# A decoder layer on one core: copies moved between two queues, the attention stage reordered, one load and one split earlier, and four down-projection inputs split ahead of the last up tile

## The chip, the cores and the metric

The kernel runs on one core of a Trainium2 chip. The metric is the device time of one execution in microseconds (us); lower is better. The engines are named as the profile names them: PE is TensorE, DVE is VectorE, ACT is ScalarE, POOL is GpSimd, SP is SyncE, which only issues DMAs here. Each engine works through its own queue in order and meets the others by semaphores.

## The reference

One layer of a hybrid decoder, 256 tokens of width 2048, in float32. Cut to what matters:

```
ada = silu(c) @ w_ada + b_ada                 # 2048 -> 6 vectors of 2048
sh_m, sc_m, gt_m, sh_f, sc_f, gt_f = split(ada, 6)
h = rmsnorm(x, g_pre_mix) * (1 + sc_m) + sh_m
q, k, v, u = split(h @ w_in)                  # 1024, 128, 128, 1024 columns
attn = sliding_window_attention(q, k, v, sinks)   # 16 heads, window 128
y = s5_ssm(u, ...)                            # a complex diagonal recurrence over time
z = gelu(y);  ssm = z * sigmoid(z @ w_glu)
mix = concat(rmsnorm(attn), rmsnorm(ssm)) @ w_out
x = x + (1 + gt_m) * rmsnorm(mix, g_post_mix)
h = rmsnorm(x, g_pre_ffn) * (1 + sc_f) + sh_f
val, gate = split(causal_conv3(h @ w_up))     # 2 x 5632 columns
ff = (gelu(gate) * val) @ w_down
x = x + (1 + gt_f) * rmsnorm(ff, g_post_ffn)
```

## The kernel before

The kernel goes through five stages: the input projection (A), the attention and recurrence stage, the gate and output projection, the up projection, the down projection. All weights stream from HBM through six buffers of 128 x 2048 floats (`raw`); SP issues these loads in the order of the program, and each waits until a buffer is free.

**Precision.** Output, up and down projections are done as three products of a high and a low part: `split(hi, lo, src, e)` casts on ScalarE (`hi`) and subtracts on VectorE, or on POOL if the second letter of `e` is g (`lo`). `hl` does this for half a weight tile (128 x 1024). In the profile the parts are h_wout and l_wout, h_wup and l_wup, h_wdn and l_wdn; fh and fl are those of a down-projection input.

**Order.** In the attention stage and up to the first up tiles the program writes the order of VectorE, ScalarE, POOL and TensorE out by hand (class `in_order`, whose call stands at line 72, so most instructions there carry L72). After `s1m.close()` a planner orders these four engines; only SP keeps the program's order.

**The attention stage.** `B(k4, kk...)` does the second half of the query projection, 64 matmuls in all over four weight tiles (16 calls of 4 matmuls, each run in two passes); `q_tiles` copies the result out. For each of eight head pairs hp: `att_scores(hp)` (TensorE), `att_max(hp)` (VectorE finds the masked maximum, ScalarE does the exponentials), `att_norm(hp)` (a tiny reciprocal on VectorE, then four scalings on ScalarE), `pv(hp)` (TensorE transposes, ScalarE copies to pT), `att_out(hp)` (TensorE, then a ScalarE copy out of PSUM bank 7). Beside it runs the recurrence: `scan(n)` does the next n of ten steps on VectorE, `x2_half` copies the states, `y_mu(yb)` and `y_cx(yb)` are its two products into one PSUM bank, `y_out(yb)` copies that out, and `z_part(n)` transposes it and applies the Gelu on ScalarE.

Also beside it, the adaLN vectors are computed: `do()` is one sum of 128 x 2048 products on VectorE (line 142) and then a `pump()`; `pair()` does two tiles with TensorE into bank 7 and copies the partial sums out (`part`); `cols()` sums these with a few matmuls in the same bank and copies two columns to `ada`. `pump(n)` issues the next n loads of a fixed list (adaLN tiles, gate weights). Both copies are on ScalarE.

**Output projection.** The loop over k loads w_out tiles and adaLN tiles, splits, multiplies, and does one or two `do()`. At k = 9 it issues the load of x1's first half, at k = 13 that of the second half and of the first up tiles. The last three k are held back, so that the banks finish one after the other.

**Start of the up projection.** Residual and norm are done in quarters (`sq`, `gain`, `x_add`), the result is transposed (`x_turn`), scaled (`x_scale`) and split (`x_split`) into h2, four tiles h2A and h2B in the profile. In between stands the split of the last half of the second up tile, `ups[1].append(hl_half(wu1, 1))`.

**Up and down projection.** 44 pairs of up tiles (`up_tile`) give 44 inputs `ffa[:, f]`. The first eleven get their shift later, by `late_sum`, which uses a row broadcast in the buffer with the tag "cbc"; the last `late_sum` runs at f = 32. The down projection then takes each f: load, split of ffa into fh and fl (tags y0 and y1, three buffers each, shared with the up tiles), split of the two weight halves, 24 matmuls.

Of the kernel before, what the change touches and what calls it, by code (L numbers as in the profile page):

```python
# [59 lines left out]
def decoder_layer(ctx: ExitStack, tc: tile.TileContext, i, out):  # L60
# [524 lines left out]
    def pair():  # L585
        (vec, m, t0), (_, _, t1) = pair_in.pop(0), pair_in.pop(0)
        ps = bank(7, "ps_ada")
        ada_mm((t0, t1), ps)
        pump(2)
        part = parts[:, npair[0] % 3]  # L590
        npair[0] += 1
        A.copy(part, ps[:, :2 * P])
        pairs.append((ps[:, 2 * P:2 * P + 2], part, vec * KD + m))

    def cols():
        res, part, o = pairs.pop(0)
        ada_cols(part, 2, res)
        A.copy(ada[:, o:o + 2], res)


    accB = []
# [174 lines left out]
    def att_norm(hp):  # L776
        st, s_ = ast[:, hp], prob[hp]
        V.tensor_add(st[:, :, 2:4], st[:, :, 2:4], st[:, :, 4:6])
        V.reciprocal(st[:, :, 2:4], st[:, :, 2:4])
        for h2 in range(2):  # L780
            for b, bs in ((0, slice(0, P)), (1, slice(P, 3 * P))):
                act_scale(s_[:, h2, bs], s_[:, h2, bs], st[:, h2, 2 + b:3 + b])

    def pv(hp, heads=(0, 1)):
        s_ = prob[hp]
        pT = pts.setdefault(hp, [])
        for h2 in heads:
            psp = bank((4, 3 if hp < 4 else 4 if hp < 6 else 6)[h2], "ps_p")
            for b in range(3):
                PE.transpose(psp[:, b * P:(b + 1) * P], s_[:, h2, b * P:(b + 1) * P], ident)  # L790
            pT.append(p2.tile([P, 3 * P], F32, tag="pT", name="pT", bufs=2))
            A.copy(pT[h2], psp[:, :3 * P])
# [102 lines left out]
    def B(k4, *kks):  # L895
        for kk in kks:
            mm_winb(k4, kk)
# [23 lines left out]
    pv(1)  # L921
    att_scores(2)
    B(1, 1)
    scan(2)
    att_max(2)
    att_out(1)
    B(1, 2, 3)
    pump()
    scan(2)
    att_norm(2)  # L930
    B(2, 0)
    pv(2)
    att_scores(3)
    scan(2)
# [5 lines left out]
    x2_half(0)  # L940
    x2_half(1)
    att_max(3)
    B(3, 0)
    y_mu(0)
    B(3, 1)
    att_norm(3)
    B(3, 2)
    do()
    pv(3)
    B(3, 3)  # L950
    pump()
    pair()
    q_tiles(2, A.copy)
    q_tiles(3, V.tensor_copy)
    y_cx(0)
    y_out(0)
    cols()
# [19 lines left out]
    y_out(2)  # L977
    att_out(4)
    att_scores(7)
    pair()  # L980
    z_part(0)
    pv(5)
# [2 lines left out]
    y_block(3, (0, 1))  # L985
    att_norm(6)
    att_out(5)
    att_max(7)
    y_block(3, (2, 3))
    y_out(3)  # L990
    pair()
# [137 lines left out]
    for k in range(3, KD):  # L1129
        while len(outs_) < min(k + 3, KD):  # L1130
            ld_out()
            ld(2 if k in (4, 6, 8) else 1)
        while nw < min(2 * k + 6, 2 * KD):
            out_hl(nw)
            nw += 1
        out_proj(k, 0)
        out_proj(k, 1)
        if 3 < k < 8:
            ssm_half(2 * k - 8)
        for _ in range(2 if k in (5, 7, 9) else 1):  # L1140
            if ada_in:
                do()
        if k == 9:

            x1 = [ld_x("x1", 0)]
        elif k == 13:
            wu0, wu1 = (raw(i["w_up"][0, vg], 2048, "wup") for vg in range(2))
            x1.append(ld_x("x1", 1))
        if G1 is None:

            g1c = p3.tile([P, KD], F32, name="g1c")
            V.tensor_add(g1c, ada[:, GT_M * KD:(GT_M + 1) * KD], bp1[:, GT_M * KD:(GT_M + 1) * KD])
            V.tensor_mul(g1c, g1c, col("g_post_mix"))
            G1 = []
        elif G1 is not None and len(G1) == 0 and k > 6:
            G1 = [dram.tile([P, KD], F32, name="g1_row")]
            nc.sync.dma_start(G1[0], g1c)
        elif G1 is not None and len(G1) == 1:
            G1.append(p3.tile([P, D], F32, name="G1"))
            nc.sync.dma_start(G1[1], dap(G1[0], 0, [[0, P], [1, D]]))  # L1160
# [6 lines left out]
    def hl_half(wu, half):  # L1167
        return hl(wu[:, half * 1024:(half + 1) * 1024], "wup", True)
# [131 lines left out]
    proj_held(acc, held, 1, 2)  # L1300
    x_turn(0, 2)
    x_turn(0, 3)
    ups[1].append(hl_half(wu1, 1))
    sq(1, 2)
    x_scale(0, 2)
    x_split(0, 2, "ag")
# [1 line left out]
    x_scale(0, 3)  # L1308
    x_split(0, 3, "av")
    rstd_start(24, nrm[:, 2, 1:2])  # L1310
    proj_held(acc, held, 1, 3)

    early = [bank(0, "ps_u"), bank(1, "ps_u")]
# [115 lines left out]
    for f in range(KF):  # L1429
        if f == LATE:  # L1430
            add_shift()
        for vg in range(2):
            n = 2 * f + vg
            if f < LATE:
                up_tile(f, vg, ffa[:, KF - 1 - f if vg else f])
            else:
                y = p4.tile([P, S], F32, tag=f"y{vg}", name=f"y{vg}", bufs=3)
                up_tile(f, vg, y)
                if vg == 0:
                    yv = y  # L1440
            if n < 2 * LATE:
                if 1 < n < 2 + KD:
                    norm_h2(n - 2)
                if n % 2 == 0 and n < KD:
                    shp = shift_pair(n)
                elif n < KD:
                    shift_cols(*shp)
                    if n == KD - 1:

                        ps = bank(6, "ps_row")  # L1450
                        PE.matmul(ps[:KD, :P], lhsT=shift[:, 1], rhs=ident, start=True, stop=True)
                        shr = p4.tile([KD, P], F32, name="shr")
                        A.copy(shr, ps[:KD, :P])
                        shbc.append(row_bcast(to_row(shr), keep.tile([P, D], F32, tag="cbc", name="shbc")))
            elif f < KF - LATE:
                for j in range((n - 2 * LATE) * 2 * LATE // (2 * KF - 4 * LATE),
                               (n + 1 - 2 * LATE) * 2 * LATE // (2 * KF - 4 * LATE)):
                    late_sum(j)
        if f >= LATE:
            A.activation(y, y, AF.Gelu_apprx_tanh)  # L1460
            V.tensor_mul(ffa[:, f], y, yv)
# [4 lines left out]
    for f in range(KF):  # L1466
        wd = raw(i["w_down"][f], 2048, "wdn")
        if f == 4:
            cbc2 = row_bcast(c_row, act.tile([P, D], F32, tag="A1", name="cbc2"))
        if f > 4 and f % 2 and f // 2 - 2 < KD:  # L1470
            ada_granule(GT_F, f // 2 - 2, cbc2)
        if f == 2 * KD + 4:

            V.tensor_add(g2c, ada[:, GT_F * KD:], bp1[:, GT_F * KD:])
            V.tensor_mul(g2c, g2c, col("g_post_ffn"))
            G2 = row_bcast(to_row(g2c), act.tile([P, D], F32, tag="A0", name="G2"))
        fh = p4.tile([P, S], F32R, tag="y0", name="fh", bufs=3)
        fl = p4.tile([P, S], F32R, tag="y1", name="fl", bufs=3)
        split(fh, fl, ffa[:, f])
        for half in range(2):  # L1480
            wh, wl = hl(wd[:, half * 1024:(half + 1) * 1024], "wdn", True)
            args = (acc, f, KF, fh, fl, wh, wl, half)
            if f < KF - 2:
                proj_tokens(*args)
            else:
                held.append(args)
# [94 lines left out]
```

## Time and profile before

| what | us |
|---|---|
| median of 3 runs | 1172.03 (1169.88 to 1173.23) |
| profiled execution, its time | 1168.57 |
| profiled execution, its span (first to last instruction) | 1166.4 |
| TensorE busy | 1124.3 (96% of the span) |
| VectorE busy | 871.2 (75%) |
| ScalarE busy | 556.3 (48%) |
| POOL busy | 92.9 (8%) |
| mean granted TensorE clock | 0.988 |
| moved by DMA | 325.87 MB, 279 GB/s on average |

Busy shares are averages over stages with different limits; a stage is read by itself. A granted clock of 1.00 is 2.4 GHz, 0.50 is 1.2 GHz. The start of a row is counted from the first instruction. A matmul's end is modelled, so neighbouring rows overlap a little.

### The profile page before, as it was taken

Reading aid. Unit: us, or ns where it says so; the run is one execution under the profiler, and the core shown is the slowest. Engines: PE = TensorE matmul, PEld = TensorE weight load, DVE = VectorE, ACT = ScalarE, POOL = GpSimd, SP = SyncE. Lnnn points to the kernel's source line nnn. Section 1 sums busy time; section 2 is a strip of 40 time slices with the busy share of each in tenths; the row PEclk is TensorE's granted clock in tenths of the full one; section 3 lists DMA queues with packets and bytes.
Section 4 is the critical chain, followed back from the end, with each engine's and each line's share of the span. In section 5 each row is a group of like instructions: output and inputs, shape, how many; then the busy total and the mean of one; then the engine's idle time right before and its main releaser. Section 6 shows DMA issues by size and latency. Waiting matters only on the chain.

```text
span 1166.4 us, 18823 instructions
## 1 busy us (share of the span) xinstructions
PE 1124.3 (96%) x7504; PEld 943.3 (81%) x7504; DVE 871.2 (75%) x1375; ACT 556.3 (48%) x943; POOL 92.9 (8%) x90
## 2 busy tenths in 40 slices
PE   7899998989998999999999999999999999999996
PEld 5788876768786888888888888888888788888885
DVE  5976938636798797569999989986676776676555
ACT  3122043564534554446766555655555444444443
POOL 5005501034000200000000000000000000000002
PEclk9999998999998999999999999999999999999998
DMA  9999977787899479986887787775555778778712
GB/s 385 381 361 356 368 258 307 290 328 280 343 354 420 147 267 350 332 307 217 289 313 284 271 299 277 286 257 192 203 181 183 285 268 294 280 276 290 261 63 73
DMA packets 49145, 325.87 MB, mean 279 GB/s; under 512 B 5521, under 2 KB 7745, under 8 KB 12449
## 3 DMA queue, kind: packets, MB, share of 16 engines
q1 hardware_dynamic: 48240, 321.06, 73.9%
q0 software_dynamic: 672, 3.55, 0.8%
q8 instruction: 59, 0.97, 0.3%
q14 instruction: 30, 0.24, 0.1%
q10 hardware_dynamic: 144, 0.05, 0.0%
HBM read 317.27 MB, written 7.37 MB: 278 GB/s over the span
## 4 chain that ended last, share of the span: by engine, by line
PE 60%; issue 23%; DVE 11%; ACT 3%; DMA 2%; POOL 1%; DVEq 0%; ACTq 0%; POOLq 0%
PE ps_u L1263 27%; PE ps_u L1265 14%; PE accA L336 5%; PE ps_ada L155 3%; DVE l_wout L72 2%; PE ps_g L1041 2%; DVE ada L142 2%; PE accB L609 2%; DVE scm L142 1%; DMA wout<-in_w_out_dram 1%; DVE scn L72 1%; PE ps_u L1252 1%; PE mix L559 1%; PE ps_wt L298 1%; PE ps_y L815 1%
## 5 line engine op out<-in xcount | busy, mean ns | idle before, releaser
L549 ACT CAST h_wup<-wup 128x1024 fp32r<-128x1024 f32 x168 | 176.5, 1052 | 194.5 <-PE ps_u L1263 176.3
L550 DVE TENSOR_TENSOR l_wup<-wup,h_wup 128x1024 fp32r<-128x1024 f32 x168 | 205.6, 1225 | 84.1 <-ACT h_wup L549 79.2
L1263 PE MATMUL ps_u<-h2B,h_wup 128*128 128x512 f32 x688 | 243.7, 395 | 0.0
L1263 PE MATMUL ps_u<-h2A,h_wup 128*128 128x512 f32 x688 | 243.5, 395 | 0.0
L1265 PE MATMUL ps_u<-h2A,l_wup 128*128 128x256 f32 x688 | 191.9, 279 | 0.0
L1265 PE MATMUL ps_u<-h2B,l_wup 128*128 128x256 f32 x688 | 191.5, 278 | 0.0
L550 DVE TENSOR_TENSOR l_wdn<-wdn,h_wdn 128x1024 fp32r<-128x1024 f32 x88 | 107.7, 1224 | 65.5 <-ACT h_wdn L549 65.5
L1263 PEld LDWEIGHTS ps_u<-h2B,h_wup 128*128 128x128 f32 x688 | 129.0, 188 | 30.3 <-issue 0.6
L1263 PEld LDWEIGHTS ps_u<-h2A,h_wup 128*128 128x128 f32 x688 | 128.9, 188 | 29.8 <-issue 0.4
L549 ACT CAST h_wdn<-wdn 128x1024 fp32r<-128x1024 f32 x88 | 92.6, 1053 | 78.7 <-PE dn L568 70.4
L1265 PEld LDWEIGHTS ps_u<-h2A,l_wup 128*128 128x128 f32 x688 | 129.4, 188 | 0.8 <-issue 0.6
L1265 PEld LDWEIGHTS ps_u<-h2B,l_wup 128*128 128x128 f32 x688 | 129.4, 188 | 0.2 <-issue 0.2
L336 PE MATMUL accA<-hT,win 128*128 128x256 f32 x448 | 108.7, 390 | 1.6 <-ACT hT L396 1.6
L568 PE MATMUL dn<-h_wdn,fl 128*128 128x512 f32 x336 | 104.6, 396 | 1.4 <-DVE fl L550 1.4
L568 PE MATMUL dn<-l_wdn,fh 128*128 128x512 f32 x336 | 105.6, 395 | 0.0
L568 PE MATMUL dn<-h_wdn,fh 128*128 128x512 f32 x336 | 105.5, 396 | 0.0
L336 PEld LDWEIGHTS accA<-hT,win 128*128 128x128 f32 x448 | 82.3, 192 | 14.3 <-issue 3.2
L142 DVE CUSTOM_DVE_ANT_0 ada<-ada,cbc 128x2048 f32<-128x2048 f32 x38 | 86.6, 2286 | 0.0
L568 PEld LDWEIGHTS dn<-h_wdn,fl 128*128 128x128 f32 x336 | 63.0, 188 | 17.0 <-DVE fl L550 1.9
L568 PEld LDWEIGHTS dn<-l_wdn,fh 128*128 128x128 f32 x336 | 63.1, 188 | 15.3
L568 PEld LDWEIGHTS dn<-h_wdn,fh 128*128 128x128 f32 x336 | 63.0, 188 | 15.2
L1419 DVE CUSTOM_DVE_ANT_0 wupt<-wupt,shbc 128x2048 f32<-128x2048 f32 x22 | 50.3, 2286 | 0.0
(357 smaller groups left out, 1553.8 us busy)
## 6 DMA issues: line engine op xcount, KB each, us to landing
wup<-in_w_up_dram SPq DMA_DIRECT2D x88, 1024.0 KB
ada<-in_w_ada_dram SPq DMA_DIRECT2D x64, 1024.0 KB
wdn<-in_w_down_dram SPq DMA_DIRECT2D x44, 1024.0 KB
wupt<-in_w_up_t_dram SPq DMA_DIRECT2D x22, 1024.0 KB
scm<-in_w_ada_dram SPq DMA_DIRECT2D x16, 1024.0 KB
shm<-in_w_ada_dram SPq DMA_DIRECT2D x16, 1024.0 KB
wout<-in_w_out_dram SPq DMA_DIRECT2D x16, 1024.0 KB
win<-in_w_in_a_dram SPq DMA_DIRECT2D x16, 896.0 KB
```

The source lines that it names most:

```text
L72: self.last = self.no_earlier(getattr(self.e, name)(*args, **kw))
L142: return nc.vector.tensor_tensor_reduce(t, t, cbc, 1.0, 0.0, ALU.mult, ALU.add, accum_out=dst)
L155: PE.matmul(ps[32 * j:32 * j + 32, v * P:(v + 1) * P], lhsT=csil[:, kc:kc + 1].to_broadcast([P, 32]), rhs=t[:, kc * P:(kc + 1) * P], start ...
L336: PE.matmul(accA[ct // 2][:, (ct % 2) * S:(ct % 2 + 1) * S], lhsT=winA[k][:, ct * P:(ct + 1) * P], rhs=hk, start=(k == 0 and ct % 2 == 0), ...
L549: (A.copy if e[0] == "a" else V.tensor_copy)(hi, src)
L550: (V if e[1] == "v" else G).tensor_sub(lo, src, hi.bitcast(F32))
L568: PE.matmul(acc[tt * 4 + half * 2 + n2], lhsT=a_[:, tk], rhs=b_[:, n2 * 512:(n2 + 1) * 512], start=(kk == 0 and first), stop=(kk == nk - 1 ...
L609: PE.matmul(accB[ct // 2][:, (ct % 2) * S:(ct % 2 + 1) * S], lhsT=wt[:, kk * 512 + ct * P:kk * 512 + (ct + 1) * P], rhs=hT[k // 8][:, k % ...
L1041: PE.matmul(psg[ct][:, :S], lhsT=wg_[ct // 2][:, (ct % 2 * 8 + k) * P:(ct % 2 * 8 + k + 1) * P], rhs=zf[:, k], start=(k == 0), stop=(k == 7))
L1263: PE.matmul(ps, lhsT=wh[:, ks], rhs=h2[kk // 4][:, kk % 4].rearrange("p a b -> p (a b)"), start=(kk == 0), stop=(kk == KD - 1), skip_group ...
L1265: PE.matmul(ps[:, :S], lhsT=wl[:, ks], rhs=h2_of(kk)[0], start=False, stop=(kk == KD - 1), skip_group_check=True)
L1419: V.tensor_tensor_reduce(t, t, shbc[0], 1.0, 0.0, ALU.mult, ALU.add, accum_out=rlate[:, vg, f:f + 1])
```

## The change

Five edits, in the order of the program:

1. In `pair()` and `cols()` the copy of the partial sums and the copy of the two columns go from ScalarE to VectorE, each at the same place of the program, and so into VectorE's queue.
2. The attention stage is reordered. Two scan steps that stood ahead of att_max(2) become one; two between att_max(2) and att_norm(2) become one; two more stand behind B(2, 0). All of B(3, ...) and its pump() come right behind att_max(3), then att_norm(3), both q_tiles, y_mu(0), pair(), do(), pv(3). att_max(7) comes right behind att_scores(7), ahead of a pair() and of z_part(0).
3. x1's first half is loaded at k = 3 instead of k = 9 of the output projection.
4. The split of the last half of the second up tile comes behind the splits of all quarters of the first 128 tokens.
5. Ahead of the last up tile, ffa[:, 0] to ffa[:, 3] are split into a buffer `fpre` with the tag "cbc", where the shift's row was; the down projection takes its first four inputs from there.

```diff
--- before.py
+++ after.py
@@ -589,13 +589,13 @@
         pump(2)
         part = parts[:, npair[0] % 3]
         npair[0] += 1
-        A.copy(part, ps[:, :2 * P])
+        V.tensor_copy(part, ps[:, :2 * P])
         pairs.append((ps[:, 2 * P:2 * P + 2], part, vec * KD + m))
 
     def cols():
         res, part, o = pairs.pop(0)
         ada_cols(part, 2, res)
-        A.copy(ada[:, o:o + 2], res)
+        V.tensor_copy(ada[:, o:o + 2], res)
 
 
     accB = []
@@ -921,14 +921,15 @@
     pv(1)
     att_scores(2)
     B(1, 1)
-    scan(2)
+    scan(1)
     att_max(2)
     att_out(1)
     B(1, 2, 3)
     pump()
-    scan(2)
+    scan(1)
     att_norm(2)
     B(2, 0)
+    scan(2)
     pv(2)
     att_scores(3)
     scan(2)
@@ -940,18 +941,15 @@
     x2_half(0)
     x2_half(1)
     att_max(3)
-    B(3, 0)
+    B(3, 0, 1, 2, 3)
+    pump()
+    att_norm(3)
+    q_tiles(2, A.copy)
+    q_tiles(3, V.tensor_copy)
     y_mu(0)
-    B(3, 1)
-    att_norm(3)
-    B(3, 2)
+    pair()
     do()
     pv(3)
-    B(3, 3)
-    pump()
-    pair()
-    q_tiles(2, A.copy)
-    q_tiles(3, V.tensor_copy)
     y_cx(0)
     y_out(0)
     cols()
@@ -977,6 +975,7 @@
     y_out(2)
     att_out(4)
     att_scores(7)
+    att_max(7)
     pair()
     z_part(0)
     pv(5)
@@ -985,7 +984,6 @@
     y_block(3, (0, 1))
     att_norm(6)
     att_out(5)
-    att_max(7)
     y_block(3, (2, 3))
     y_out(3)
     pair()
@@ -1140,7 +1138,7 @@
         for _ in range(2 if k in (5, 7, 9) else 1):
             if ada_in:
                 do()
-        if k == 9:
+        if k == 3:
 
             x1 = [ld_x("x1", 0)]
         elif k == 13:
@@ -1300,7 +1298,6 @@
     proj_held(acc, held, 1, 2)
     x_turn(0, 2)
     x_turn(0, 3)
-    ups[1].append(hl_half(wu1, 1))
     sq(1, 2)
     x_scale(0, 2)
     x_split(0, 2, "ag")
@@ -1308,6 +1305,7 @@
     x_scale(0, 3)
     x_split(0, 3, "av")
     rstd_start(24, nrm[:, 2, 1:2])
+    ups[1].append(hl_half(wu1, 1))
     proj_held(acc, held, 1, 3)
 
     early = [bank(0, "ps_u"), bank(1, "ps_u")]
@@ -1429,6 +1427,11 @@
     for f in range(KF):
         if f == LATE:
             add_shift()
+        if f == KF - 1:
+
+            fpre = keep.tile([P, 4, 2, S], F32R, tag="cbc", name="fpre")
+            for f2 in range(4):
+                split(fpre[:, f2, 0], fpre[:, f2, 1], ffa[:, f2])
         for vg in range(2):
             n = 2 * f + vg
             if f < LATE:
@@ -1474,9 +1477,12 @@
             V.tensor_add(g2c, ada[:, GT_F * KD:], bp1[:, GT_F * KD:])
             V.tensor_mul(g2c, g2c, col("g_post_ffn"))
             G2 = row_bcast(to_row(g2c), act.tile([P, D], F32, tag="A0", name="G2"))
-        fh = p4.tile([P, S], F32R, tag="y0", name="fh", bufs=3)
-        fl = p4.tile([P, S], F32R, tag="y1", name="fl", bufs=3)
-        split(fh, fl, ffa[:, f])
+        if f < 4:
+            fh, fl = fpre[:, f, 0], fpre[:, f, 1]
+        else:
+            fh = p4.tile([P, S], F32R, tag="y0", name="fh", bufs=3)
+            fl = p4.tile([P, S], F32R, tag="y1", name="fl", bufs=3)
+            split(fh, fl, ffa[:, f])
         for half in range(2):
             wh, wl = hl(wd[:, half * 1024:(half + 1) * 1024], "wdn", True)
             args = (acc, f, KF, fh, fl, wh, wl, half)
```

## Rows read from the trace of the kernel before

**Rows 1.** The page's first part (busy time and share of the span, instructions of each engine), and then three stretches of the engines' busy time by stage: the stretch and its length, busy us of PE, PEld, DVE, ACT and POOL with their instructions, the granted TensorE clock, the mean busy share of the 16 DMA engines, GB/s.

```profile
PE 1124.3 (96%) x7504; PEld 943.3 (81%) x7504; DVE 871.2 (75%) x1375; ACT 556.3 (48%) x943; POOL 92.9 (8%) x90
...
300.00:330.00 30.00, 30.00 (x135) 24.60 (x134) 25.38 (x33) 13.92 (x18) 0.23 (x1) 1.00 0.87 330
350.00:360.00 10.00, 10.00 (x46) 8.29 (x45) 9.80 (x10) 4.01 (x4) 0.00 (x0) 1.00 1.01 424
520.00:900.00 380.00, 380.00 (x2191) 332.19 (x2190) 318.92 (x494) 225.32 (x355) 0.00 (x0) 1.00 0.70 251
```

**Rows 2.** The list of what TensorE waited for over the whole span: what waited, for what, us in total, how often, the longest.

```profile
PE ps_p L790 <- ACT s__1646 L72: 5.6, 1, 5.6
...
PE mix L559 <- ACT h_wout L72: 3.0, 1, 3.0
...
PE ps_u L1252 <- POOL h2B L72: 1.5, 1, 1.5
...
PE dn L568 <- DVE fl L550: 1.4, 1, 1.4
```

**Rows 3.** TensorE in order of time, 155 to 270 us: start, us, line, operation, tiles, shapes, count, and in brackets the idle time before and what ended it. Line 609 is a B matmul, 790 pv's transposes, 828 y_cx.

```profile
184.77 5.45 PE L609 MATMUL accB<-hT,winb 128*128 128x256 f32 x24
195.79 1.78 PE L790 MATMUL ps_p<-c,s__1646 128*128 128x128 f32 x6 [5.57 <-ACT s__1646 L72]
...
199.08 2.80 PE L609 MATMUL accB<-hT,winb 128*128 128x256 f32 x8
...
217.89 1.97 PE L828 MATMUL ps_y<-Z,X2A 128*64 128x128 f32 x32
```

**Rows 4.** VectorE in order of time, around the scan. scn and Vs belong to scan steps, s__1646 to att_max(2), ast to the softmax's small columns, X2A to x2_half.

```profile
188.82 0.33 DVE L72 CUSTOM_DVE_ANT_0 s__1646<-ps_s,mask,c 128x128 f32<-128x128 f32 x1
...
190.35 1.13 DVE L72 TENSOR_TENSOR scn<-Vs,scn 128x256 f32<-128x256 f32 x2
...
194.84 0.17 DVE L72 TENSOR_TENSOR ast<-ast 128x4 f32<-128x4 f32 x1
...
195.15 1.10 DVE L72 TENSOR_TENSOR scn<-Vs,scn 128x256 f32<-128x256 f32 x2
...
205.89 0.42 DVE L72 COPY X2A<-Vs 64x512 f32<-64x512 f32 x1
```

**Rows 5.** ScalarE in order of time: the first exponential of att_max(2), and the four scalings of att_norm(3).

```profile
190.48 0.40 ACT L72 ACTIVATE s__1646<-s__1646,ast 128x128 f32<-128x128 f32 x1 [8.71 <-DVE ast L72]
...
211.09 1.49 ACT L72 ACTIVATE s__1762<-s__1762,ast 128x128 f32<-128x128 f32 x4 [0.50 <-DVE ast L72]
```

**Rows 6.** Short stretches: in the first row the stretch, TensorE's busy us and instructions, the granted clock, DMA share, GB/s; the second row has all engines, as in the first group.

```profile
194.00:196.00 2.00, 0.21 (x1) 0.50 1.03 430
...
368.00:376.00 8.00, 6.94 (x18) 5.15 (x19) 7.09 (x11) 5.81 (x9) 0.00 (x0) 0.57 1.00 410
```

**Rows 7.** TensorE in order of time, the second half of the attention stage: line 162 is the matmuls of cols(), 155 those of a pair, 790 pv's transposes.

```profile
231.33 0.61 PE L162 MATMUL ps_ada<-sel,parts 128*128 128x1 f32 x4
...
237.78 1.95 PE L155 MATMUL ps_ada<-ada,csil 128*32 128x128 f32 x64 [0.76 <-ACT qT L72]
...
242.51 0.55 PE L790 MATMUL ps_p<-c,s__1943 128*128 128x128 f32 x3 [1.86 <-ACT pT L72]
...
253.31 1.95 PE L155 MATMUL ps_ada<-ada,csil 128*32 128x128 f32 x64 [1.64 <-ACT ada L72]
```

**Rows 8.** ScalarE in order of time, same stage: the first exponential of att_max(6), a table load and the Gelu of z_part(0) behind it, a further table load.

```profile
233.85 0.40 ACT L72 ACTIVATE s__2057<-s__2057,ast 128x128 f32<-128x128 f32 x1
...
240.19 1.28 ACT L72 ACT_TABLE_LOAD   x1
241.49 0.60 ACT L72 ACTIVATE zT<-ps_z 128x512 f32<-128x512 f32 x1
...
246.56 1.28 ACT L72 ACT_TABLE_LOAD   x1
```

**Rows 9.** VectorE in order of time, same stage: att_norm(4), the ada sum of a do(), att_norm(5).

```profile
227.25 0.15 DVE L72 TENSOR_TENSOR ast<-ast 128x4 f32<-128x4 f32 x1
...
227.56 2.29 DVE L142 CUSTOM_DVE_ANT_0 ada<-ada,cbc 128x2048 f32<-128x2048 f32 x1
...
231.32 0.15 DVE L72 TENSOR_TENSOR ast<-ast 128x4 f32<-128x4 f32 x1
```

**Rows 10.** Output projection: SyncE's queue (the load of x1's first half), ScalarE (the casts of the last w_out tile), and the list of what VectorE waited for from 340 to 371 us.

```profile
340.98 0.43 SPq L110 DMA_DIRECT2D x<-in_x_dram  x1
...
367.50 1.99 ACT L72 CAST h_wout<-wout 128x1024 fp32r<-128x1024 f32 x2 [3.05 <-DMA wout<-in_w_out_dram]
...
DVE l_wout L72 <- ACT h_wout L72: 0.7, 2, 0.5
DVE hl_wout L72 <- ACT hl_wout L72: 0.3, 1, 0.3
```

**Rows 11.** Start of the up projection: VectorE's split of half an up tile, and POOL's subtractions for h2A and h2B, each in order of time.

```profile
387.53 2.12 DVE L72 TENSOR_TENSOR l_wup<-wup,h_wup 128x1024 fp32r<-128x1024 f32 x1 [1.63 <-ACT h_wup L72]
...
386.03 2.53 POOL L72 TENSOR_TENSOR h2A<-prod,h2A 128x512 fp32r<-128x512 f32 x2 [5.30 <-ACT h2A L72]
390.98 1.26 POOL L72 TENSOR_TENSOR h2B<-prod,h2B 128x512 fp32r<-128x512 f32 x1 [2.41 <-ACT h2B L72]
```

**Rows 12.** Start of the down projection: VectorE's low part of the first down input.

```profile
913.24 0.42 DVE L550 TENSOR_TENSOR fl<-ffa,fh 128x256 fp32r<-128x256 f32 x1
```

## The prediction

> **What bounds the kernel now.** I read the page's first part, then the engines' busy time by stage, then the list of what TensorE waited for. TensorE is busy 96% of the span, and from 520 to 900 us for all of 380 us, where VectorE is busy 319 and ScalarE 225 [rows 1]. In that stage only TensorE's own work counts, and the diff leaves that as it is. So the change can pay only where TensorE waits or runs at the lower clock. The list names four long waits at places that the diff touches: 5.6 us in the attention stage, 3.0 before the last output-projection weights, 1.5 at the first up tile, 1.4 at the first down tile [rows 2]. Each is then read on the engines that end it.
>
> **The 5.6 us wait.** TensorE finishes B(2,0) at 184.77 + 5.45 = 190.2 and starts pv(2) at 195.79 [rows 3], 0.95 after VectorE's att_norm(2) at 194.84 (ScalarE's scaling lies between). On VectorE two scan steps stand between att_max(2) at 188.82 and that norm: 190.35 to 194.84, 2.25 each [rows 4]. The change leaves one step ahead of att_max(2) and one behind it. So att_max(2) comes a step earlier, about 186.5; ScalarE's exponentials, which began at 190.48 [rows 5], begin near 188.2 and take 2.2; the one step behind att_max(2) ends near 190.4 as well. att_norm(2) comes at 190.4 and pv(2) at 191.3: the wait is 1.1 us, **4.5** less.
>
> The old wait cost a second time. The granted clock reads 0.50 in 194 to 196 us [rows 6], which is 1.2 GHz, after TensorE had been idle from 190.2. Eight B matmuls took 2.80 there, where 24 took 5.45 before [rows 3]. The work from 195.79 to 199.08 + 2.80 = 201.9 needs about 3.9 at full clock (pv(2) is also paced by ScalarE), so 2.2 more is lost. Behind a wait of 1.1 I expect full clock: behind the 1.64 us wait at 253.31 a pair takes 1.95, as at 237.78 [rows 7]. Together 6.7.
>
> **What is late next.** The scan still has ten steps. After 190.7 six are left, where four were left after 195.15; those four ended at 205.89 [rows 4], and two more narrow ones of 2.3 give 190.7 + 4.6 + 10.7 = 206.0. So X2, att_max(3) and att_norm(3) come when they did, within 0.2: ScalarE scales tile 3 at about 211.3 instead of 211.09, for 1.49 [rows 5]. TensorE, with all of B(3), y_mu(0) and pair() ahead of pv(3), is busy from 191.3 for pv(2) 1.3, scores 0.9, 56 B matmuls at 5.45/24 = 12.7, att_out 0.8, y_mu 2.0 and the pair's 1.95: until 210.9. pv(3) then waits about 0.9 and is paced by ScalarE to 213.05. y_cx(0) follows there instead of at 217.89 [rows 3]: **4.8** of the 6.7 remain. The pump() calls that move with B(3) and pair() ask for their loads some 5 us sooner, as the buffers come free sooner; SP's queue gets no new wait.
>
> **The copies that go to VectorE** cost little by themselves (bounds 0.15, its row of four columns [rows 9], and 0.42, its 512-column copy at 205.89 [rows 4]; I take 0.4, nearer in size). They cost through the queue. Today VectorE does att_norm(4) at 227.25 and do() at 227.56 without waiting for cols() [rows 9]. Now the two-column copy stands ahead of do(), att_max(6) and att_norm(5), and ScalarE waits for those. With all 4.8 earlier, TensorE's cols() runs at 231.33 − 4.8 = 226.5 [rows 7] and ends at 227.1; do() (2.29) and att_max(6) (1.5) then end near 231.0, where 231.32 − 4.8 = 226.5 would have done [rows 9]. ScalarE's exponentials of tile 6 began at 233.85 [rows 8], less 4.8 is 229.0; they now begin at 231.1. By these 2.1 slips the copy of att_out(4), which frees the bank of the third pair: TensorE starts that pair near 235.2 instead of 237.78 − 4.8 = 233.0. **2.2 is given back**, and the wait there grows from 0.76 [rows 7] to about 3.0.
>
> **att_max(7) ahead of the first z_part** puts its exponentials with the others. The table load at 246.56 goes, and the one that returns to Gelu behind it; the one at 240.19 stays [rows 8]. The 1.86 us wait at 242.51 stays too: the same exponentials now stand ahead of that pT copy. What goes is the 1.64 at 253.31, which ended with ScalarE's two-column copy [rows 7], late behind the table load, a Gelu and two pT copies. On VectorE it is ready at once; the last part copy then stands behind a do(), 0.5. Net **1.1** won. The middle gives 4.8 − 2.2 + 1.1 = **3.7**; bounds 0 (every later pair loses as the third) and 6.5 (the third loses little).
> The Trainium skill (ScalarE: Activation LUTs, What ACT_TABLE_LOAD costs) prices a switch at 2.66 us: a load of 1.28 and a drain of 1.38. The trace shows the load without a drain: it ends at 240.19 + 1.28 = 241.47 and the Gelu starts at 241.49 [rows 8]. By the page two switches less could give 2.8 more, a total of 1161.6; the row decides.
>
> **x1 at k = 3.** In 350 to 360 us the transfers run at 424 GB/s with the DMA engines always busy, in 300 to 330 at 330 [rows 1]; a megabyte takes 2.45 us at 424. x1's first half is issued at 340.98, ahead of the last four w_out loads, and the last of them lands at 367.5, when ScalarE can start [rows 10]. Without x1 ahead it lands near 365. But VectorE is full as well: from 340 to 371 it waits only 0.7 + 0.3 = **1.0** us in all, each time for the cast of such weights [rows 10]. That is my price; bounds 0 and 2.45. At k = 3, near 310 us, there is room for the megabyte, it needs none of the six raw buffers, and its place held kdz, which is last read in the attention stage, so SP does not stop at it. The clock of 0.57 in 368 to 376 [rows 6] I leave as it is, since the wait ahead of it loses only 1.0; plus or minus 2.9, half of its stretch.
>
> **l_wup moved.** VectorE's split for the second up tile takes 2.12 beside POOL's own subtraction, and the scale that h2B needs stands behind it; POOL is free at 386.03 + 2.53 = 388.56 but starts h2B at 390.98 and ends at 392.24 [rows 11], and TensorE waits 1.5 [rows 2]. Without the split ahead, the scale comes near 386.6, ScalarE's cast ends near 387.9, and POOL works from 388.6 to 389.9, before TensorE asks at 392.24 − 1.5 = 390.7. Gain **1.5**, bounds 0.9 and 1.9. The split itself then runs near 390.6; its first reader comes some 4 us later, behind two half tiles.
>
> **The first four down splits.** VectorE's fl of the first tile starts at 913.24 [rows 12], behind an ada sum, and TensorE waits 1.4 for it [rows 2]. The eight small operations (0.4 each) now stand ahead of the last up tile, beside TensorE work without a gap. Their buffer was last read by late_sum, ten tiles earlier. Gain **1.4**, bounds 0 and 1.4: this stage is ordered by the planner, which may put something else last.
>
> **Sum.** 3.7 + 1.0 + 1.5 + 1.4 = 7.6. The profiled run took 1168.57 (span 1166.4); 7.6 less is 1161.0. The median of the three runs lies 3.5 above it, so I forecast 1172.0 − 7.6 = **1164.4**, own range 1161 to 1168. Everything from 520 to 900 is bound by TensorE and carries the gain on.
>
> **Rivals.** (A) VectorE's queue gives the whole middle back, each later pair losing like the third. For it: the copies wait for TensorE in an in-order queue. Against: only the third pair has ScalarE's exponentials and the bank close behind. 1172.0 − 3.9 = 1168.1. (B) The loads absorb the middle: TensorE arrives 3.7 earlier at a stage whose transfers run at 424 GB/s. Then x1's 2.45 and the later 2.9 count: 1166.7. Against: the loads are asked for by VectorE's releases, which move too. (C) The clock does better: the third pair loses nothing (2.2) and the low stretch at 368 goes (2.9): 1159.3. (D) The splits don't end the wait at the down projection, because the planner puts another operation last: 1165.8. (E) Slower. The place is the third pair: its wait grows to 3 us and TensorE falls to 1.2 GHz behind it, as behind the 3.0 us wait [rows 2, 6]; the copies then queue further, 2.2 at each of five pairs and 2.9 for the clock, 13.9 against 4.8 + 3.9: 1177.2. It decides once the pairs lose more than 8.7 together.
> The Trainium skill (TensorE: Matmul & The Clock Gate, HAM oscillation) describes a kernel that was throttled anew by each of its waits; here, so far, the long waits show it and the 1.64 us one doesn't.
>
> **Chances.** Forecast 0.50, A 0.15, B 0.10, C 0.17, D 0.04, E 0.04. About 0.3% (3.5 us) is what a measurement of this kernel can tell from no change. Faster: 0.48 of the forecast, half of A, most of B, C and D, 0.85; within 0.3%: 0.11; slower: 0.04. The range, 1157.5 to 1170.0, leaves out E, the upper edge of A and the far side of C.
>
> **What would show it.** Right: pv(2) waits about 1 us and the clock is 1.00 in 194 to 200; a new wait of 2 to 3 us at the third pair; one table load instead of three between the scores and the gate; the last w_out lands 2 to 3 us sooner beside a VectorE with no idle time; no wait at h2B or fl. Wrong: a clock of 0.50 in the middle, a scan that ends later, w_out landing as late as now, or idle time of TensorE between 520 and 900.

## The result, and the profile after

The changed kernel takes 1161.69 us (median of 4 executions, 1160.81 to 1162.89), the kernel before 1170.95 (4 executions, 1169.60 to 1173.23). The ratio is 0.9934, 95% interval 0.9922 to 0.9946, which is 7.7 us less (6.3 to 9.1). The forecast was 7.6 less. As a time it was 1164.4, which is 2.7 above the measured median: it was taken from the median of the three earlier executions, 1172.03. The two medians above differ by 9.3. The profiled execution took 1160.81 (span 1158.9); the sum of the terms had put it at 1161.0. So the size of the gain was right. The rows below show that two of its terms were not, and that their errors cancelled.

The busy times and two of the stretches of [rows 1] with the one of [rows 6], and then four short stretches of TensorE alone (its busy time, granted clock, DMA share, GB/s):

```profile
PE 1121.8 (97%) x7504; PEld 942.6 (81%) x7504; DVE 873.2 (75%) x1385; ACT 551.2 (48%) x931; POOL 94.8 (8%) x90
```

```profile
350.00:360.00 10.00, 10.00 (x46) 8.29 (x45) 10.00 (x11) 3.54 (x5) 0.00 (x0) 1.00 1.01 425
368.00:376.00 8.00, 8.00 (x32) 6.47 (x31) 6.13 (x11) 4.25 (x9) 0.00 (x0) 0.85 1.00 413
520.00:900.00 380.00, 380.00 (x2192) 332.12 (x2191) 319.61 (x498) 227.37 (x360) 0.26 (x1) 1.00 0.69 250
```

```profile
194.00:196.00 2.00, 2.00 (x18) 1.00 0.60 147
234.00:237.00 3.00, 2.74 (x52) 0.50 0.00 0
254.00:257.00 3.00, 3.00 (x9) 0.56 1.03 434
367.00:370.00 3.00, 2.78 (x7) 0.50 0.99 374
```

The clock of 0.50 at the old long wait [rows 6] is gone, and the stretch at 368 is half as long. But there are two new stretches at 1.2 GHz, at 234 and at 254 us. TensorE in order of time shows what stands ahead of them (columns as in [rows 3]):

```profile
181.00 1.99 PE L609 MATMUL accB<-hT,winb 128*128 128x256 f32 x8
183.73 5.45 PE L609 MATMUL accB<-hT,winb 128*128 128x256 f32 x24
190.28 1.53 PE L790 MATMUL ps_p<-c,s__1642 128*128 128x128 f32 x6 [1.10 <-ACT s__1642 L72]
...
212.22 1.97 PE L828 MATMUL ps_y<-Z,X2A 128*64 128x128 f32 x32
...
234.26 3.42 PE L155 MATMUL ps_ada<-ada,csil 128*32 128x128 f32 x64 [2.92 <-ACT qT L72]
...
239.32 0.55 PE L790 MATMUL ps_p<-c,s__1943 128*128 128x128 f32 x3 [0.73 <-ACT pT L72]
...
248.73 1.95 PE L155 MATMUL ps_ada<-ada,csil 128*32 128x128 f32 x64 [0.25 <-DVE ada L72]
...
252.10 0.61 PE L162 MATMUL ps_ada<-sel,parts 128*128 128x1 f32 x4 [0.84 <-DVE parts L72]
...
253.80 3.26 PE L1039 MATMUL ps_g<-zT,wglu 128*128 128x256 f32 x8 [0.59 <-ACT zT L72]
...
261.28 3.72 PE L1039 MATMUL ps_g<-zT,wglu 128*128 128x256 f32 x16 [0.62 <-ACT pT L72]
```

**How to compare.** I take the start of the same matmul in both traces. The B block at 183.73 began at 184.77 before [rows 3]: 1.04 sooner, although both programs are the same up to there. That 1.04 is chance of this execution (a short stretch at the lower clock in another place), so it is taken off everything that follows. pv(2) starts 195.79 − 190.28 − 1.04 = 4.47 sooner by the change, y_cx(0) 4.63, the third pair 237.78 − 234.26 − 1.04 = 2.48, the fifth pair 3.54, and the 16 gate matmuls at 261.28, which began at 262.39 before, 262.39 − 261.28 − 1.04 = 0.07. In this execution the middle won 4.6 us and had nothing left of it at 261 us.

Behind the gate the late edits show on the engines that end the old waits (in order of time, one fence each for TensorE, ScalarE and POOL):

```profile
365.59 0.50 PE L559 MATMUL mix<-h_wout,mh 128*128 128x512 f32 x1 [1.73 <-ACT h_wout L72]
367.22 0.79 PE L559 MATMUL mix<-l_wout,mh 128*128 128x512 f32 x1 [1.13 <-DVE l_wout L72]
...
903.21 0.62 PE L568 MATMUL dn<-h_wdn,fpre 128*128 128x512 f32 x2
```

```profile
364.49 2.00 ACT L72 CAST h_wout<-wout 128x1024 fp32r<-128x1024 f32 x2 [3.04 <-DMA wout<-in_w_out_dram]
```

```profile
385.03 1.30 POOL L72 TENSOR_TENSOR h2B<-prod,h2B 128x512 fp32r<-128x512 f32 x1
```

The last w_out tile is there at 364.49 instead of 367.50 [rows 10]; of these 3.0 us, 1.6 is the shift that TensorE already has ahead of it (364.82 before, 363.24 now). POOL starts h2B without idle time instead of after 2.41 [rows 11], and the first down matmul follows the last up matmul at once; nothing waits for fl [rows 2, 12].

### The profile page after: what moved, and what is told of

Same layout as the page of the kernel before. It is cut to its first block, busy times and chain, and to the rows that moved or that the text cites. A ratio compares the mean times of both kernels' runs of the same rounds, so it can differ in the third digit from the quotient of the medians.

```text
span 1158.9 us, 18810 instructions
## 1 busy us (share of the span) xinstructions
PE 1121.8 (97%) x7504; PEld 942.6 (81%) x7504; DVE 873.2 (75%) x1385; ACT 551.2 (48%) x931; POOL 94.8 (8%) x90
## 4 chain that ended last, share of the span: by engine, by line
PE 78%; DVE 9%; issue 7%; ACT 3%; DMA 1%; POOL 1%; DVEq 0%; POOLq 0%; ACTq 0%
PE ps_u L1261 28%; PE dn L568 15%; PE ps_u L1263 14%; PE accA L336 8%; PE ps_ada L155 4%; DVE l_wout L72 2%; DVE ada L142 2%; PE ps_g L1039 2%; PE mix L559 1%; DVE scn L72 1%; DMA shm<-in_w_ada_dram 1%; PE ps_u L1250 1%; PE ps_wt L298 1%; PE ps_y L828 1%; PE ps_ada L162 1%
## 5 line engine op out<-in xcount | busy, mean ns | idle before, releaser
L568 PE MATMUL dn<-l_wdn,fh 128*128 128x512 f32 x304 | 95.8, 396 | 0.0
L568 PE MATMUL dn<-h_wdn,fl 128*128 128x512 f32 x304 | 95.8, 396 | 0.0
L568 PE MATMUL dn<-h_wdn,fh 128*128 128x512 f32 x304 | 95.8, 395 | 0.0
L568 PEld LDWEIGHTS dn<-h_wdn,fl 128*128 128x128 f32 x304 | 57.1, 188 | 13.9
L568 PEld LDWEIGHTS dn<-h_wdn,fh 128*128 128x128 f32 x304 | 57.1, 188 | 13.8
L568 PEld LDWEIGHTS dn<-l_wdn,fh 128*128 128x128 f32 x304 | 57.1, 188 | 13.8
```

Of the source, the lines that this page charges most:

```text
L568: PE.matmul(acc[tt * 4 + half * 2 + n2], lhsT=a_[:, tk], rhs=b_[:, n2 * 512:(n2 + 1) * 512], start=(kk == 0 and first), stop=(kk == nk - 1 ...
```

## The experiments

Two theories stood against each other from here. **S** is the recorded sum: the middle is worth 3.7, the late edits 3.9, and the stretches at the lower clock in the profile are chance. **Q** says that VectorE's queue, with a pair's copies in it, gives most of the middle back, partly through the clock behind its waits, and that the late edits are worth more than I put down. Each kernel ran beside the kernel before on the same chip; the ratio is to that. In the diffs, minus is the changed kernel, unless said otherwise.

**The late edits alone** (the kernel before, with x1's early loads, l_wup's place and the four early splits; in this diff the kernel before is the base, and it is cut to one or two lines of each edit):

```diff
-        if k == 9:
+        if k == 3:
             x1 = [ld_x("x1", 0)]
...
     rstd_start(24, nrm[:, 2, 1:2])
+    ups[1].append(hl_half(wu1, 1))
...
+        if f == KF - 1:
+            fpre = keep.tile([P, 4, 2, S], F32R, tag="cbc", name="fpre")
```

> The kernel before with the three late edits alone (early x1 loads, l_wup's place, the four inputs of the down projection split ahead). Theory Q: the late edits are worth 5 to 6 us: 1165 to 1166. Theory S: 3.9 us: 1167.1.

Measured 1163.46, ratio 0.9953 (0.9932 to 0.9973): 5.5 us less, 3.2 to 8.0. **The middle alone** is the changed kernel with those three hunks undone.

> The changed kernel without its three late edits: the middle alone. Theory Q: 0 to 2 us gained: 1169 to 1171. Theory S: 3.7 us: 1167.3.

Measured 1168.21, ratio 0.9988 (0.9971 to 1.0005): 1.4 us less, between 3.4 less and 0.6 more. In its profile the gate matmuls start at 261.26, 0.02 later than before once the chance shift is off. As gains, both medians are on Q's side; as times they lie 1.5 and 0.8 below Q's ranges, since the kernel before took 1169.68 beside them. The first interval still holds S's 3.9; the second just excludes its 3.7, and so does the trace.

**Both copies of a pair back on ScalarE**, and then each one by itself:

```diff
-        V.tensor_copy(part, ps[:, :2 * P])
+        A.copy(part, ps[:, :2 * P])
...
-        V.tensor_copy(ada[:, o:o + 2], res)
+        A.copy(ada[:, o:o + 2], res)
```

> The changed kernel with both of its moved copies (scan copy and column copy) back on ScalarE; the late edits stay. Theory Q (VectorE's queue and the lower clock behind its waits eat the gain at the scan): the third pair's wait falls from 2.9 to about 1 us and the low-clock stretch behind it goes, the scan's waits go back to 5.6 and 4.8 us; the whole lands at 1159 to 1162, no slower than the changed kernel's 1161.7. Theory S (the recorded sum: the middle is worth 3.7): 1165.4, that is 3.7 slower than the changed kernel.

Measured 1159.33, ratio 0.9916 (0.9892 to 0.9940): not slower than the changed kernel but 2.4 faster by the medians. The two intervals overlap, so no gain of the copies on VectorE is seen, and S's 3.7 us of loss is outside the interval. One line of my own expectation was wrong: no copy of a pair stands in the scan, and the scan's gain stays whole (pv(2) at 190.28 with a wait of 1.09). The third pair's wait fell as expected, to 0.76, but another came in its place (TensorE, then ScalarE):

```profile
232.10 1.95 PE L155 MATMUL ps_ada<-ada,csil 128*32 128x128 f32 x64 [0.76 <-ACT qT L72]
...
238.05 0.90 PE L790 MATMUL ps_p<-c,s__1943 128*128 128x128 f32 x3 [3.08 <-ACT pT L72]
...
259.00 3.29 PE L1039 MATMUL ps_g<-zT,wglu 128*128 128x256 f32 x14 [0.62 <-ACT pT L72]
```

```profile
235.37 0.35 ACT L72 COPY parts<-ps_ada 128x256 f32<-128x256 f32 x1
235.74 1.28 ACT L72 ACT_TABLE_LOAD   x1
237.03 0.60 ACT L72 ACTIVATE zT<-ps_z 128x512 f32<-128x512 f32 x1
237.52 0.47 ACT L72 COPY pT<-ps_p 128x384 f32<-128x384 f32 x1
```

pv(5)'s second half now waits 3.08 instead of 0.73 for a copy that stands on ScalarE behind the last exponentials, a pair's copy, a table load and a Gelu. So the 2.15 at the third pair were no net loss: with the queue open there, nearly the same time is waited at the next place. What the copies on VectorE cost in waits is the end of the stage: here there is no wait at the last pair or the gate. 2.36 of the gain reach 259.00 instead of 0.07, although this execution has 6.8 us at the lower clock behind the 3.08 (from 237.3), as much as the two stretches at 234 and 254 together.

> The changed kernel with only the large copy of a pair (128x256) back on ScalarE; the two-column copy stays on VectorE. Theory Q, if the two-column copy that waits for the small matmuls is what holds VectorE's queue at the third pair: that wait stays at 2.9 us and the low-clock stretch behind it too, the wait ahead of the gate (0.84 and 0.59) goes: 1160 to 1161. If the large copies' time on VectorE does it: the third pair's wait falls towards 1 us and the time to 1159.5, as with both copies back. Theory S: no gain against the changed kernel.

> The changed kernel with only the two-column copy back on ScalarE; the large copy stays on VectorE. Theory Q, if the two-column copy is what holds VectorE's queue: the third pair's wait falls to about 1 us, its low-clock stretch goes, the wait ahead of the gate stays: 1159 to 1160.5. If the large copy does it: 2.9 us of wait and 1161.7. Theory S: 1.3 us slower than the changed kernel, 1163.

The large copy back: 1163.92, ratio 0.9952 (0.9936 to 0.9968). The two-column copy back: 1160.38, ratio 0.9921 (0.9902 to 0.9941). Four rows decide it, two of the first kernel and two of the second:

```profile
236.04 3.61 PE L155 MATMUL ps_ada<-ada,csil 128*32 128x128 f32 x64 [3.01 <-ACT qT L72]
257.79 0.61 PE L162 MATMUL ps_ada<-sel,parts 128*128 128x1 f32 x4 [2.24 <-ACT parts L72]
```

```profile
232.96 1.95 PE L155 MATMUL ps_ada<-ada,csil 128*32 128x128 f32 x64 [0.75 <-ACT qT L72]
238.66 0.55 PE L790 MATMUL ps_p<-c,s__1943 128*128 128x128 f32 x3 [2.83 <-ACT pT L72]
```

The two-column copy is the one that holds the queue: with it on VectorE both waits are there (and with the large copy on ScalarE the last pair's even grows, to 2.24), with it on ScalarE both are gone, whatever engine has the large copy. Two lines of these expectations did not come. With the large copy back, the wait ahead of the gate was to go and the time to be 1160 to 1161: the 0.59 went, but the 0.84 became 2.24. ScalarE's copy stands there at 257.39 behind the scalings of att_norm(7) at 255.99, and these wait for VectorE's norm at 255.18, behind the do() at 252.87 and the two-column copy at 252.80. With the two-column copy back, the wait ahead of the gate was to stay, and it went.

**Without the early split**, and **with x1's loads late again** (the two hunks undone, one in each kernel):

> The changed kernel without the early split of the first four inputs of the down projection: each is split in its turn, as before. The wait of 1.4 us at the start of the down projection comes back, and the first 96 matmuls go at 233.3 instead of 226.8 ns (0.6 us): 2.1 to 2.4 slower than the changed kernel, 1164. By the recorded term (the wait alone) 1163.1.

> The changed kernel with the loads of x1 back in their old place, late among the output projection's loads. The recorded term: 1.0 us slower (bounds 0 to 2.45, the clock's stretch left aside), 1162.7; its profile shows the waits for the last w_out tiles at 3.8 us in place of 2.9. With the second half of the low-clock stretch at 368 to 375 us back as well, 0.9 more: 1163.6.

1163.67 and 1163.05, ratios 0.9950 (0.9938 to 0.9962) and 0.9932 (0.9912 to 0.9953): by the medians 2.0 and 1.4 slower than the changed kernel's 1161.69, though both intervals overlap its own. In the traces the start of the down projection is worth 2.3 in the one; in the other the stretch from 362 to 392 us is 2.1 longer, of which 0.9 goes with a stretch at the lower clock of 6.8 instead of 3.4 us. That 0.9 can't be put down to x1: the stretch is 6.8 us in all three profiles with the late loads, but also in four of the eleven with the early ones. This is one of the four, the copies-back kernel (columns as in the short stretches above):

```profile
364.00:370.00 6.00, 5.25 (x12) 0.50 0.93 345
```

**The spacing of the down matmuls.** In the changed kernel the first 96 down matmuls, which use fpre, start 226.7 ns apart, the later ones 233.3, as all did before. The compiled program puts fpre, and the operands of the output projection, which also go at 227, at 384 bytes past a multiple of 512 in their partition; the weights beside them lie there too. The later fh and fl start 416 past one. Three kernels move them by 32, 96 and 992 bytes with a larger small tensor ahead of them:

```diff
-rlate = p4.tile([P, 2, LATE], F32
+rlate = p4.tile([P, 2, 16], F32
...
+rlate = p4.tile([P, 2, LATE + 12], F32
...
+rlate = p4.tile([P, 2, LATE + 124], F32
```

> The changed kernel with one small tensor on chip padded, so that the split inputs of the down projection made after the up tiles lie 64 bytes aligned in their partition like the first four, which show 226.7 ns a matmul where the later ones show 233.5. If the address sets the spacing: all down matmuls run at about 226.7, the 960 left gain 6.5 us, 1155.2. If it is something else about the first four (their early making): the spacing stays at 233.5 and the time at 1161.7.

> The changed kernel with one small tensor padded by 96 bytes, so that the split inputs of the down projection that are made behind the up tiles begin at a multiple of 128 bytes in their partition (at a multiple of 64 in the last such run, which left the spacing at 233.3 ns). The tensors of the up and the output projection and the first four inputs, whose matmuls go at 226.7 or its equal, all begin at a multiple of 128. If that is what sets the spacing: all 1056 matmuls of the down projection at about 227 ns, 960 x 6.6 ns = 6.3 us less than the changed kernel, 1155.4 against its 1161.7. If something else about the first four sets it: 233.3 ns and 1161.7 as before.

> The changed kernel with both copies of a pair back on ScalarE, and one small tensor padded by 992 bytes, so that the later split inputs of the down projection begin at 384 past a multiple of 1024 bytes, the place in 1024 that the first four, the weights beside them and the mix have; starts at multiples of 64 and 128 left the spacing at 233.3 and 232.4 ns. If the place relative to the weights sets the spacing: 227 ns in all of the down projection and 6.3 us less than the 1159.3 with the copies back, 1153. If it is not the address: 232 to 233.5 ns and 1159.3.

(The third one has both copies of a pair back on ScalarE as well.) The first gave 1162.85, ratio 0.9955 (0.9930 to 0.9979), the second 1162.07, 0.9938 (0.9913 to 0.9962): no gain, spacing 233.3 and 232.4. The third gave **1154.71**, ratio 0.9859 (0.9837 to 0.9881), 4.6 less than its neighbour with the copies back by the medians, 6.7 by the ratios. TensorE around 1000 us, first in the changed kernel, then in the third; the starts of successive pairs of matmuls are 0.47 apart, then 0.45 to 0.46:

```profile
999.66 0.63 PE L568 MATMUL dn<-l_wdn,fh 128*128 128x512 f32 x2
1000.13 0.63 PE L568 MATMUL dn<-h_wdn,fl 128*128 128x512 f32 x2
1000.60 0.63 PE L568 MATMUL dn<-h_wdn,fh 128*128 128x512 f32 x2
```

```profile
999.99 0.62 PE L568 MATMUL dn<-h_wdn,fl 128*128 128x512 f32 x2
1000.44 0.62 PE L568 MATMUL dn<-h_wdn,fh 128*128 128x512 f32 x2
1000.90 0.39 PE L568 MATMUL dn<-l_wdn,fh 128*128 128x512 f32 x1
```

TensorE's matmuls from 950 to 1090 us, in the changed kernel, after the move by 96 and after the move by 992 bytes:

```profile
950.00:1090.00 140.00, 140.00 (x602) 1.00 0.78 285
```

```profile
950.00:1090.00 140.00, 140.00 (x604) 1.00 0.78 287
```

```profile
950.00:1090.00 140.00, 140.00 (x620) 1.00 0.79 290
```

The first two guesses (a multiple of 64, of 128) fell; the third, the same place as the weights, held over the whole projection.

**pv(5) ahead of the last maximum and the first z part**, with both copies back:

```diff
     att_scores(7)
-    att_max(7)
     pair()
-    z_part(0)
     pv(5)
+    att_max(7)
+    z_part(0)
     cols()
```

> The changed kernel with both copies of a pair back on ScalarE, and at the third pair the last head pair's maximum with its four exponentials, and the first z part with its table load, put behind pv(5). With the copies back, pv(5)'s second half waits 3.08 us for a copy queued on ScalarE behind those exponentials, a pair's copy, the table load and a Gelu. Theory Q: that wait falls to 0.6 to 1.0 us and the low-clock stretch behind it (6.8 us from 237.6) goes or shrinks: 2 to 5 us less than the 1159.3, 1154.5 to 1157.5. Against it: the next wait at ScalarE's queue (fourth or fifth pair, the gate's first input) takes it back, 1159.3.

Measured 1157.85, ratio 0.9889 (0.9865 to 0.9913): 1.5 less than with the copies back alone, just above the range expected, and the two intervals overlap, so this gain is not clear of the noise. The profiled execution took 1164.2 and is 6 above that median because its up matmuls stand 2% farther apart from 570 us on; up to the gate it can be read:

```profile
236.18 0.55 PE L790 MATMUL ps_p<-c,s__1943 128*128 128x128 f32 x3 [0.62 <-ACT pT L72]
...
241.44 0.88 PE L801 MATMUL ps_o<-pT,vtok 128*64 128x128 f32 x12 [1.87 <-ACT ada L72]
...
257.45 3.72 PE L1039 MATMUL ps_g<-zT,wglu 128*128 128x256 f32 x16 [0.62 <-ACT pT L72]
```

The 3.08 us wait is 0.62, and 1.87 of it comes back at att_out(5), behind the table load. **With the move by 992 bytes as well:**

> The last two together: the changed kernel with both copies of a pair back on ScalarE, pv(5) ahead of the last maximum and the first z part, and the 992 bytes of padding. The address alone brought 1159.3 to 1154.7, the order at pv(5) brought 1159.3 to 1157.9; they touch different stages, so their gains add: 1153.3, between 1151.5 and 1155. If the gain at pv(5) was chance: 1154.7.

**1150.41**, ratio 0.9845 (0.9810 to 0.9880), 11 us less than the changed kernel and the fastest of all. The median is 2.9 below the two gains added, and what made it so is not known; by the ratios they add within the interval (0.9916 less 0.0057 for the address and 0.0027 for the order is 0.9832).

## Why the prediction came out

Net gain of TensorE's start at five places, chance shift ahead of the change taken off, in the profiled executions (the changed kernel's middle is in five other kernels too: four agree with it within 0.1 everywhere; the fifth, the move by 96 bytes, agrees within 0.2 up to the gate's first matmul, has no stretch at the lower clock there and keeps 1.59 at the last place):

| kernel | y_cx(0) | third pair | fifth pair | gate, first matmul | gate, 16 matmuls |
|---|---|---|---|---|---|
| forecast | 4.8 | 2.6 | 4.2 | 3.7 | 3.7 |
| the change | 4.63 | 2.48 | 3.54 | 1.85 | 0.07 |
| two-column copy back | 4.62 | 4.64 | 4.80 | 4.75 | 4.72 |
| both copies back | 4.64 | 4.65 | 2.36 | 2.36 | 2.36 |
| both back, pv(5) first | 4.62 | 4.64 | 4.92 | 4.92 | 4.92 |

Each row is one execution, and the lower clock falls differently in each. The copies-back kernel has its 6.8 us behind the third pair; the kernels of the third and the fifth row have none there, but 3.4 us near 193, ahead of y_cx(0). So the 2.36 beside 4.72 and 4.92 is mostly the clock of these executions and no ranking of the kernels; their medians are 1159.33, 1160.38 and 1157.85.

**The scan, right.** pv(2) waits 1.10 (forecast 1.1), the clock behind it is 1.00, 4.63 are left at y_cx(0) against 4.8. The scan is indeed late next, and the copies have no part in this. The clock part of the 6.7 was 1.8 and not 2.2 (the work from pv(2) to att_out takes 194.51 − 190.28 = 4.23, where 3.9 had been put down), which changes nothing, since the scan is later. "Behind a wait of 1.1 I expect full clock" held here and in nine other profiles with this order, and failed in two, where the stretch near 193 us stands behind the same wait (the two-column copy back):

```profile
194.00:196.00 2.00, 2.00 (x6) 0.50 0.67 188
```

Even there 4.62 are left at y_cx(0): pv(3), which waits 1.07 in the changed kernel, then doesn't wait at all.

**The third pair, right in size and cause, wrong in what it means.** 2.15 given back against 2.2, wait 2.92 against 3.0, through the queue as told (VectorE, then ScalarE):

```profile
226.30 0.16 DVE L72 COPY ada<-ps_ada 128x2 f32<-128x2 f32 x1 [2.73 <-PE ps_ada L162]
226.45 2.29 DVE L142 CUSTOM_DVE_ANT_0 ada<-ada,cbc 128x2048 f32<-128x2048 f32 x1
...
228.67 0.35 DVE L72 CUSTOM_DVE_ANT_0 s__2057<-ps_s,mask,c 128x128 f32<-128x128 f32 x1
```

```profile
230.34 0.40 ACT L72 ACTIVATE s__2057<-s__2057,ast 128x128 f32<-128x128 f32 x1 [2.06 <-DVE ast L72]
```

The copies-back kernel shows that nearly the same time is waited at pv(5) in any case. And the sum has no cost for the clock behind the 3.0 us wait that it forecasts itself; only rival E has one. Behind that wait the pair takes 3.42 instead of 1.95, which is 1.47 lost. The fifth pair is still near its forecast, because another term was wrong the other way: "The 1.86 us wait at 242.51 stays too", but it is 0.73. With the 1.64 that became 0.25, 2.48 + 1.13 + 1.39 − 1.47 = 3.53.

**The step that failed** is "the last part copy then stands behind a do(), 0.5. Net 1.1 won." The last pair's copy stands behind the two-column copy, that do() and att_norm(7), and att_norm(7) itself is late by the same queue (VectorE, then ScalarE, where the Gelu for the gate stands behind the scalings of att_norm(7)):

```profile
248.51 0.16 DVE L72 COPY ada<-ps_ada 128x2 f32<-128x2 f32 x1 [1.13 <-PE ps_ada L162]
248.59 2.45 DVE L142 CUSTOM_DVE_ANT_0 ada<-ada,cbc 128x2048 f32<-128x2048 f32 x1
...
250.97 0.56 DVE L72 TENSOR_TENSOR ast<-ast 128x4 f32<-128x4 f32 x1
...
251.66 0.39 DVE L72 COPY parts<-ps_ada 128x256 f32<-128x256 f32 x1
```

```profile
251.78 1.49 ACT L72 ACTIVATE s__2106<-s__2106,ast 128x128 f32<-128x128 f32 x4 [2.91 <-DVE ast L72]
253.17 1.06 ACT L72 ACTIVATE zT<-ps_z 128x512 f32<-128x512 f32 x2
```

It costs 0.84 at the last pair and 0.59 at the gate, 3.54 − 1.85 = 1.69 in all where 0.5 had been put down, and then, in five of the six profiles with this middle, 1.78 of lower clock. So the middle's 3.7 is 0.1 to 1.6 in the traces and 1.4 by its own kernel: rival A's outcome, by two places and the clock, not by each pair in turn.

**The late edits were put too low**, 3.9 against 5.5 (3.2 to 8.0). l_wup's place is right: 1.6 in the trace against 1.5. x1 gains 1.1 ahead of the clock, against 1.0; the lower-clock stretch behind it is 3.4 instead of 6.8 us, 0.9 more in this execution, but not surely by the edit (four kernels with the early loads show 6.8). The prediction had left that at plus or minus 2.9. The first down tiles gain 2.3, not 1.4: the starts of their 96 matmuls span 21.80 instead of 24.09 us, of which the wait is 1.7 measured from start to start, and 96 × 6.6 ns = 0.63 is the faster spacing, which nothing in the trace before had shown for this stage. In the sum 2.3 to 3.6 too much in the middle met 1.1 to 2.0 too little behind (without and with the clock's 0.9); the right total was luck to that extent. In the profiled execution the final matmuls start 7.48 sooner. 1.04 of that is the chance shift, and about 0.5, won in small steps between the gate and 365 us, belongs to no term.

## What to carry to other kernels

A copy that is nearly free by its duration can be dear by its place: a 0.16 us copy that must wait for TensorE, ahead of a norm and an ada sum in an in-order queue, cost more by the medians (1163.9 with it alone on VectorE, 1160.4 with the other alone) than the 0.4 us copy that the change was also moving. When a stage gets faster, follow the gain through every later wait to the last matmul of the stage before booking it; the rows here show 4.6, 2.5, 3.5 and 0.1 within 45 us. And compare two traces by the shift of the same matmul, with the shift from ahead of the change taken off, or chance of a microsecond passes for an effect. A stretch at the lower clock in one trace is part of that chance: look whether other profiles with the same code have it, before it is booked.

## What the hardware showed that was not expected

**The place of the stationary operand.** Starts at 416, 448, 0 and 384 bytes past a multiple of 512 gave 233.3, 233.3, 232.4 and 226.7 ns a matmul (128x128 stationary, 512 columns moving, full clock). 384 is where the moving weights start, and whether the place in itself counts or the one relative to the weights was not told apart. The two token halves of an input begin 512 bytes apart, and in the kernel with 992 bytes the matmuls of both start 226 to 227 ns after the one before; so the pattern repeats with 512 bytes or with 256, and not with 128, by which 0 and 384 would be alike. Over 960 matmuls it is 6.4 us, as much as most of this change. As it stands it is no rule for other stages: the up projection, which the second expectation counted among the fast ones, has both operands at 384 too, and there a matmul of 512 columns and one of 256 together take 346 ns (1155 matmuls in 200 us), not 1.5 × 226.7 = 340. Why the place counts is not shown.

**The lower clock behind waits is not a matter of the longest wait alone.** A stretch at 1.2 GHz came with the waits of 2.9 to 3.0 at the third pair in all seven profiles that have them, and with both of 3.08 at pv(5), but not with the one of 2.83 there; behind 1.87 at att_out(5) it came in one kernel and not in the other; behind the 0.84 and 0.59 at the gate it came in five of six. And it is not fixed by the kernel: all fourteen programs are the same up to the 1.55 us wait at 166 us, and a stretch of 3.4 us follows it in four of their profiles, the kernel before among them (granted clock 0.58 in 166 to 170 us), and not in the other ten. The Trainium skill (TensorE: Matmul & The Clock Gate, HAM oscillation) describes a kernel that each of its waits throttles again. The rows agree for the third pair, and only in part for the rest.

**A table load without a drain.** In the copies-back kernel the load ends at 235.74 + 1.28 = 237.02 and the Gelu starts at 237.03. The Trainium skill (ScalarE: Activation LUTs, What ACT_TABLE_LOAD costs) adds a drain of 1.38; again no row has it.

**Not explained:** the 2% wider spacing of the up matmuls in one execution; the other five of that program took 1156.45 to 1161.26.
